# A 4-layer hybrid diffusion step in fp32 halves: the order of the products in the first blocks

## Chip, cores, metric

One Trainium2 chip, one core. The metric is the time of one execution of the program on the device, in microseconds, as the median over runs.

## What is computed

One inference step of 384 tokens (128 context tokens, 256 latent ones) with 1024 channels through four layers. Layer l mixes tokens with a bidirectional Mamba-2 scan (l = 0, 3), a gated short convolution (l = 1) or differential attention (l = 2), and then runs a gated convolutional FFN. Each half of a layer is normed before and after, and shifted, scaled and gated by a modulation vector:

```python
def sandwich_layer(x, mod, g, mix_fn, ffn_fn):
    sh1, sc1, gt1, sh2, sc2, gt2 = jnp.split(mod, 6, axis=-1)
    m, aux = mix_fn(rmsnorm(x, g[0]) * (1 + sc1) + sh1)
    x = x + gt1 * rmsnorm(m, g[1])
    f = ffn_fn(rmsnorm(x, g[2]) * (1 + sc2) + sh2)
    x = x + gt2 * rmsnorm(f, g[3])
    return x, aux

def conv_ffn(h, w_up, conv_w, w_down):
    u = dwconv(h @ w_up, conv_w)
    gate, val = jnp.split(u, 2, axis=-1)
    return (jax.nn.silu(gate) * val) @ w_down
```

The argument of mix_fn and ffn_fn is called h here.

## The kernel before

**Two parts.** Matrix products are made in a rounded 32-bit format. To keep the accuracy, every operand is split in two parts, a first part (its rounded value) and a second part (what the rounding left). A product is then three matmuls: first × first, first of the weight × second of h, second of the weight × first of h. The first part of h is hh, the second hl; those of a weight chunk are wh and wl.

**How h is made.** h is channel-major: two tiles of four 128-channel blocks for hh and two for hl, each over all 384 tokens. It comes in three token tiles of 128 (t = 0, 1, 2). For each, normed (line 278) makes the normalised tile xn, turned (288) transposes its eight blocks on TensorE, and modulated (298) scales and shifts them into h32, four blocks at a time: three on ACT (L309), the fourth on VectorE (L307). A cast on VectorE (L311) makes hh, and a subtraction (L312) makes hl. The second half's subtraction runs on POOL for t = 0 and 1; all others run on VectorE. There are HB = 2 buffers of h32 (four before layer 0).

**How weights come.** wplan lists all weight chunks in the order of use. ahead (141) loads them (four raw buffers wr), rounds a chunk on ACT (L155, wh) and subtracts on VectorE (L156, wl); WS = 4 chunks of parts are held. A chunk has 1024 columns: four channel blocks by two output blocks of 128 in the FFN, two chunks for a pair of output blocks; in the short convolution 768 columns, four chunks for three output blocks. dt of the scan has one chunk of 512 columns, all eight channel blocks by 64 outputs.

**Channel-major phases.** The scan's input projections, the short convolution's and the FFN's upward product write channels on the partitions and the 384 tokens along the free axis. cm_block (330) makes one output block: it goes through the chunks and channel blocks, and for each issues the three matmuls (L340) into one bank of PSUM, 24 in all (dt: 24 with 64 columns). FFN and short convolution have five banks (mm), the scan three and two (mm, yp). An FFN step (i = 0 to 21) makes two blocks, gate and value, each of which goes through conv (393: ACT L396, VectorE L398 and L400). The short convolution makes three blocks per step. The scan makes dt first (steps, 536), then pairs of blocks. Attention takes its projections token-major (L811) and does not use cm_block.

**What lies between phases.** tm_out (353) makes the product at the end of each half layer; as soon as a token tile is finished, it takes the residual, the norm and the next h for it, so the last tile's norm, transposes, h and cast stand between one phase's products and the next's. The modulation products (modps, L187) for later layers are spread over the program as filler on TensorE, and their weights (w_mod) come through the same DMA queue.

**What sets the order.** Everything is issued by one Python program, but the context is made with schedule_with_timeline_sim=True: at build time, instructions are put in order on each engine by an estimate of when their inputs are ready, with the program's order as priority. On the chip each engine then runs its list in order.

Of the kernel before, what the change touches and what calls it, by code (L numbers as in the profile page):

```python
# [10 lines left out]
F32 = mybir.dt.float32  # L11
# [3 lines left out]
ALU = mybir.AluOpType  # L15
# [4 lines left out]
P = 128  # L20
D = 1024
KB = D // P
T = 384
# [21 lines left out]
class Net:  # L45
# [252 lines left out]
    def modulated(self, l, which, t, trs):  # L298

        o, n = TOK[t]  # L300
        hh, hl = self._h4
        for hf, tr in enumerate(trs):
            h32 = self.op.tile([P, 4, P], F32, tag="h32", name="h32", bufs=self.hbufs)
            for b in range(4):
                A, B = self.ab(l, which, hf * 4 + b, COND[t])
                if b == 3:
                    self.V.tensor_scalar(h32[:, b, :], tr[:, b, :], A, B, op0=ALU.mult, op1=ALU.add)  # L307
                else:
                    self.S.activation(h32[:, b, :], tr[:, b, :], AF.Identity, scale=A, bias=B)  # L309
            hi, lo = hh[hf][:, :, o:o + n], hl[hf][:, :, o:o + n]  # L310
            self.V.tensor_copy(hi, h32)  # L311
            (self.GP if hf == 1 and t < 2 else self.V).tensor_tensor(lo, h32, hi.bitcast(F32), op=ALU.subtract)  # L312

    def gated(self, t, hf, acc, gt, parts):

# [15 lines left out]
    def cm_block(self, chunks, nblk, b, m=P, tag="mm"):  # L331

        acc = self.psum(tag)[:, :T]
        ops = []
        for k0, nk, hi, lo in chunks:
            for k in range(nk):
                o = (k * nblk + b) * m
                ops += [(hi[:, o:o + m], self.hh[k0 + k]), (hi[:, o:o + m], self.hl[k0 + k]), (lo[:, o:o + m], self.hh[k0 + k])]
        for n, (w, h) in enumerate(ops):
            self.PE.matmul(acc[:m], w, h, start=n == 0, stop=n == len(ops) - 1)  # L340
        return acc

    def cm_weights(self, nblk, m=P):
        per = max(1, 1024 // (nblk * m))
        out = []
        for k in range(0, KB, per):
            nk = min(per, KB - k)
            out.append((k, nk) + tuple(self.weights(nk * nblk * m)))
        return out
# [112 lines left out]
    def ffn(self, l, pl, then):  # L462
        d = self.d
        cw = pl.tile([P, 2 * NF, 3], F32, name="fcw")
        self.load(cw, d["ffn_conv"][l])
        g = [pl.tile([P, T], F32, name=f"fg{i}") for i in range(NF)]
        with self.tc.tile_pool(name=f"up{l}", bufs=1, reuse_waits="tile") as self.cpool:
            self.cbufs = 7
            for i in range(NF):
                ch = self.cm_weights(2)  # L470
                pg = self.cm_block(ch, 2, 0)
                pv = self.cm_block(ch, 2, 1)
                tg = self.conv(pg, cw[:, i])
                tv = self.conv(pv, cw[:, NF + i])
                self.S.activation(tg, tg, AF.Silu)
                self.V.tensor_tensor(g[i], tg, tv, op=ALU.mult)
                self.pace("ffn", i + 1, NF)

        def prep(k):
            hi = pl.tile([P, T], F32R, tag="gh", name="gh", bufs=RB)  # L480
            lo = pl.tile([P, T], F32R, tag="gl", name="gl", bufs=RB)
            self.split(g[k], hi, lo)
            return hi, lo

        self.tm_out(l, 1, NF, prep, then=then, room=1)

    def short(self, l, pl, then):
        d = self.d
        cw = pl.tile([P, KB, 3], F32, name="scw")
        self.load(cw, d["sc_conv"])  # L490
        hi = [pl.tile([P, T], F32R, name=f"sgh{i}") for i in range(KB)]
        lo = [pl.tile([P, T], F32R, name=f"sgl{i}") for i in range(KB)]
        self.cpool, self.cbufs = pl, 7
        for i in range(KB):
            ch = self.cm_weights(3)
            pc = self.cm_block(ch, 3, 0)
            pu = self.cm_block(ch, 3, 1)
            pb = self.cm_block(ch, 3, 2)
            cg = self.cpool.tile([P, T], F32, tag="c", name="cg", bufs=self.cbufs)
            self.S.activation(cg, pc, AF.Copy)  # L500
            self.V.tensor_tensor(cg, pu, cg, op=ALU.mult)
            t = self.conv(cg, cw[:, i])
            self.V.tensor_tensor(t, pb, t, op=ALU.mult)
            self.split(t, hi[i], lo[i])
            self.pace("mix", i + 1, KB)
        self.tm_out(l, 0, KB, lambda k: (hi[k], lo[k]), then=then, room=4)
# [31 lines left out]
    def steps(self, j, keep, pl, between):  # L538
# [4 lines left out]
        self.load(prm[:, 1], d["ssd_a_log"][j].partition_broadcast(P))  # L543
        na = pl.tile([P, 64], F32, name="na")
        wh, wl = self.weights(512)
        ps = self.cm_block([(0, KB, wh, wl)], 1, 0, 64)
        raw = pl.tile([64, T], F32, name="dtr")
        V.tensor_copy(raw, ps[:64])
        tr = self.pt.tile([P, 4, P], F32, tag="tp", name="tp")
# [30 lines left out]
        for dr, tri in ((0, self.Ur), (1, self.Lr)):  # L580
            ps = self.pt.tile([P, 512], F32, tag="tp", name="cum")
# [442 lines left out]
```

## Time and profile before

| | us |
|---|---|
| median of 3 runs | 2418.07 |
| lowest and highest run | 2415.47, 2423.82 |
| the profiled execution | 2415.22 |
| its span, first to last instruction | 2413.4 |
| TensorE (PE) busy | 2298.8 |
| VectorE (DVE) busy | 1618.8 |
| ScalarE (ACT) busy | 1252.9 |
| GpSimd (POOL) busy | 329.6 |

All times within the execution count from the start of the span. PE is TensorE's matmuls and PEld its weight loads, which overlap them; SP is the queue that issues DMAs. L340 is line 340 of the kernel before. Matmuls are pipelined, so their durations overlap: the distance of two starts is what one costs. mm<-hl,wh is a matmul that writes a tile mm and reads hl and wh. The mean granted clock of TensorE was 0.975 of full speed. The channel-major phases begin at 44.7 (scan of layer 0), 444.8 (its FFN), 741.2 (short convolution), 908.6 (its FFN), 1449.0 (FFN after attention), 1741.9 (scan of layer 3) and 2129.7 (its FFN).

### The profile page before, as it was taken

To read this page: it belongs to the slowest core of one execution; us is meant where nothing else is said; L and a number is where in the kernel's file an instruction comes from. 1 tells how busy PE (TensorE), PEld (TensorE's weight loads), DVE (VectorE), ACT (ScalarE), POOL (GpSimd) and SP (SyncE) were. 2 spreads that over 40 slices of the span, in tenths; PEclk is the share of its full clock that TensorE was granted. 3 is DMA by queue.
4 is the path that set the end of the run, shared out by engine and by line. 5 is a ranking of instruction groups with operands and counts; after the bars stand their busy time and mean duration, and the time that the engine had idled before them with its cause. 6 is when DMAs were issued, how large, how long until landed. Compare 5 with 4: busy or idle time off the path is not lost.

```text
span 2413.4 us, 35660 instructions
## 1 busy us (share of the span) xinstructions
PE 2298.8 (95%) x13132; PEld 2003.8 (83%) x13132; DVE 1618.8 (67%) x2930; ACT 1252.9 (52%) x2173; POOL 329.6 (14%) x498
## 2 busy tenths in 40 slices
PE   6989999899999999999999979999998999989998
PEld 3878887699977969998788649998687888779987
DVE  3887886677655457776655547776578888677765
ACT  3766765444444344444544444445556676554444
POOL 1222230100000010000133330000113223110000
PEclk7999999999999999999999989999999999989999
DMA  7656655533537563335435463345455654423342
GB/s 286 193 164 201 208 195 175 197 123 131 165 105 304 200 247 126 123 127 161 162 107 176 151 241 107 123 130 158 147 165 166 199 167 150 134 97 123 131 145 83
DMA packets 113375, 391.79 MB, mean 162 GB/s; under 512 B 13105, under 2 KB 25521, under 8 KB 100913
## 3 DMA queue, kind: packets, MB, share of 16 engines
q1 hardware_dynamic: 113200, 389.52, 48.7%
q8 instruction: 103, 1.69, 0.3%
q14 instruction: 72, 0.58, 0.1%
HBM read 382.39 MB, written 7.08 MB: 161 GB/s over the span
## 4 chain that ended last, share of the span: by engine, by line
PE 79%; DVE 9%; DMA 4%; ACT 2%; issue 2%; POOL 2%; SPq 0%; DVEq 0%; POOLq 0%; ACTq 0%
PE mm L340 44%; PE mm L380 20%; PE mm L811 5%; PE modps L187 2%; PE yp L380 2%; DVE e L686 2%; DMA wm<-in_w_mod 2%; DVE wl L156 1%; PE yp L726 1%; DVE w L690 1%; PE yp L852 1%; ACT jk L263 1%; DMA wx<-in_w_mod 1%; DVE cv L398 1%; DMA h<-in_state 1%
## 5 line engine op out<-in xcount | busy, mean ns | idle before, releaser
L340 PE MATMUL mm<-hh,wh 128*128 128x384 f32 (+1 forms) x2352 | 796.1, 340 | 15.2 <-DVE cv L400 9.5
L340 PE MATMUL mm<-hl,wh 128*128 128x384 f32 (+1 forms) x2352 | 793.9, 338 | 0.0
L340 PE MATMUL mm<-hh,wl 128*128 128x384 f32 (+1 forms) x2352 | 791.2, 338 | 0.0
L156 DVE TENSOR_TENSOR wl<-wr,wh 128x1024 fp32r<-128x1024 f32 (+2 forms) x466 | 564.0, 1212 | 259.7 <-ACT wh L155 257.6
L155 ACT ACTIVATE wh<-wr 128x1024 fp32r<-128x1024 f32 (+2 forms) x466 | 483.7, 1039 | 320.5 <-PE mm L340 258.2
L340 PEld LDWEIGHTS mm<-hh,wh 128*128 128x128 f32 (+1 forms) x2352 | 442.8, 189 | 38.8 <-DVE cv L400 14.5
L340 PEld LDWEIGHTS mm<-hl,wh 128*128 128x128 f32 (+1 forms) x2352 | 442.8, 188 | 4.6 <-issue 2.4
L340 PEld LDWEIGHTS mm<-hh,wl 128*128 128x128 f32 (+1 forms) x2352 | 442.2, 188 | 5.0 <-issue 3.3
L396 ACT ACTIVATE cv<-mm,fcw 128x384 f32<-128x384 f32 x176 | 100.1, 572 | 233.1 <-PE mm L340 228.2
L380 PE MATMUL mm<-wh,gh 128*128 128x512 f32 x528 | 208.7, 395 | 0.0
L380 PE MATMUL mm<-wl,gh 128*128 128x512 f32 x528 | 208.6, 395 | 0.0
L380 PE MATMUL mm<-wh,gl 128*128 128x512 f32 x528 | 207.9, 395 | 0.0
L271 POOL TENSOR_SCALAR m<-s 128x1 f32<-128x1 f32 x42 | 17.5, 417 | 1144.4 <-ACT jk L263 1143.6
L398 DVE SCALAR_TENSOR_TENSOR cv<-mm,fcw,cv 128x127 f32<-128x127 f32 x352 | 144.2, 410 | 42.6 <-ACT cv L396 42.6
L405 ACT ACTIVATE gh<-fg 128x384 fp32r<-128x384 f32 x176 | 92.1, 524 | 152.5 <-PE mm L380 151.6
L406 DVE TENSOR_TENSOR gl<-fg,gh 128x384 fp32r<-128x384 f32 x176 | 97.6, 557 | 96.8 <-ACT gh L405 96.1
L400 DVE SCALAR_TENSOR_TENSOR cv<-mm,fcw,cv 128x127 f32<-128x127 f32 x352 | 146.0, 416 | 10.8
L380 PEld LDWEIGHTS mm<-wh,gh 128*128 128x128 f32 x528 | 99.0, 187 | 24.8 <-issue 0.8
L380 PEld LDWEIGHTS mm<-wh,gl 128*128 128x128 f32 x528 | 99.0, 187 | 24.4
L380 PEld LDWEIGHTS mm<-wl,gh 128*128 128x128 f32 x528 | 99.0, 187 | 24.0
L187 PE MATMUL modps<-wm,sil 128*32 128x512 f32 x496 | 78.1, 654 | 15.7 <-DMA wm<-in_w_mod 14.7
L811 PE MATMUL mm<-wh,hh 128*128 128x256 f32 x288 | 83.4, 290 | 0.0
(224 smaller groups left out, 3169.0 us busy)
## 6 DMA issues: line engine op xcount, KB each, us to landing
wr<-in_ffn_up SPq DMA_DIRECT2D x176, 512.0 KB
wm<-in_w_mod SPq DMA_DIRECT2D x62, 1024.0 KB
wr<-in_ssd_in SPq DMA_DIRECT2D x96, 512.0 KB
wr<-in_ffn_down SPq DMA_DIRECT2D x88, 512.0 KB
wx<-in_w_mod SPq DMA_DIRECT2D x34, 1024.0 KB
ab<-acs SPq DMA_DIRECT2D x48, 512.0 KB
wr<-in_ssd_out SPq DMA_DIRECT2D x32, 512.0 KB
wr<-in_sc_in SPq DMA_DIRECT2D x32, 384.0 KB
```

The source lines that it names most:

```text
L155: self.S.activation(hi[:, :m], raw[:, :m], AF.Copy)
L156: self.V.tensor_tensor(lo[:, :m], raw[:, :m], hi[:, :m].bitcast(F32), op=ALU.subtract)
L187: self.PE.matmul(acc[32 * j:32 * j + 32, :], self.sil[:, kb, :], raws[:, j // 2, (j % 2) * 512:(j % 2 + 1) * 512], start=kb == 0, stop=kb ...
L340: self.PE.matmul(acc[:m], w, h, start=n == 0, stop=n == len(ops) - 1)
L380: self.PE.matmul(acc[t], g[:, o:o + n], w, start=k == 0 and i == 0, stop=k == nk - 1 and i == 2)
L396: self.S.activation(t, src, AF.Copy, scale=cw[:, 1:2])
L398: self.V.scalar_tensor_tensor(t[:, o + 1:o + n], src[:, o:o + n - 1], cw[:, 0:1], t[:, o + 1:o + n], op0=ALU.mult, op1=ALU.add)
L400: self.V.scalar_tensor_tensor(t[:, o:o + n - 1], src[:, o + 1:o + n], cw[:, 2:3], t[:, o:o + n - 1], op0=ALU.mult, op1=ALU.add)
L405: self.S.activation(hi, src, AF.Copy)
L406: self.V.tensor_sub(lo, src, hi.bitcast(F32))
L686: V.scalar_tensor_tensor(e[:, sl], abs_[t][:, 0, sl], dac[:, t, hs:hs + 1], abs_[t][:, 1, sl], op0=ALU.subtract, op1=ALU.min)
L811: PE.matmul(acc[t][:, :256], h[k][:, o:o + m], w[:, ws], start=k == 0 and i == 0, stop=k == KB - 1 and i == 2)
```

## The change

A new function cm_first makes all output blocks of a phase's first step together. It takes chunk by chunk, and in a chunk block by block, the products with hh (wh·hh, then wl·hh for each channel block); only then, block by block, all products with hl. It is used for dt in the scan, for step 0 of the FFN and step 0 of the short convolution. All other steps use cm_block as before. In modulated, the two subtractions of a token tile are issued after both casts instead of each behind its cast; this holds wherever h is made, ahead of attention too.

```diff
@@ modulated
         o, n = TOK[t]
         hh, hl = self._h4
+        subs = []
         for hf, tr in enumerate(trs):
...
             hi, lo = hh[hf][:, :, o:o + n], hl[hf][:, :, o:o + n]
             self.V.tensor_copy(hi, h32)
-            (self.GP if hf == 1 and t < 2 else self.V).tensor_tensor(lo, h32, hi.bitcast(F32), op=ALU.subtract)
+            subs.append((self.GP if hf == 1 and t < 2 else self.V, lo, h32, hi))
+        for e, lo, h32, hi in subs:
+            e.tensor_tensor(lo, h32, hi.bitcast(F32), op=ALU.subtract)
@@ new, after cm_block
+    def cm_first(self, chunks, nblk, m=P, tags=None):
+
+        accs = [self.psum((tags or ["mm"] * nblk)[b])[:, :T] for b in range(nblk)]
+        cols = lambda k, b: slice((k * nblk + b) * m, (k * nblk + b + 1) * m)
+        for k0, nk, hi, lo in chunks:
+            for b in range(nblk):
+                for k in range(nk):
+                    for w in (hi, lo):
+                        self.PE.matmul(accs[b][:m], w[:, cols(k, b)], self.hh[k0 + k], start=k0 + k == 0 and w is hi, stop=False)
+        for b in range(nblk):
+            for k0, nk, hi, lo in chunks:
+                for k in range(nk):
+                    self.PE.matmul(accs[b][:m], hi[:, cols(k, b)], self.hl[k0 + k], start=False, stop=k0 + k == KB - 1)
+        return accs
@@ ffn
-                pg = self.cm_block(ch, 2, 0)
-                pv = self.cm_block(ch, 2, 1)
+                pg, pv = self.cm_first(ch, 2) if i == 0 else [self.cm_block(ch, 2, b) for b in range(2)]
@@ short
-            pc = self.cm_block(ch, 3, 0)
-            pu = self.cm_block(ch, 3, 1)
-            pb = self.cm_block(ch, 3, 2)
+            pc, pu, pb = self.cm_first(ch, 3) if i == 0 else [self.cm_block(ch, 3, b) for b in range(3)]
@@ steps
-        ps = self.cm_block([(0, KB, wh, wl)], 1, 0, 64)
+        ps, = self.cm_first([(0, KB, wh, wl)], 1, 64)
```

## Rows read from the trace of the kernel before

**Rows 1.** The page, part 1: busy time of the engines and share of the span.
```profile
PE 2298.8 (95%) x13132; PEld 2003.8 (83%) x13132; DVE 1618.8 (67%) x2930; ACT 1252.9 (52%) x2173; POOL 329.6 (14%) x498
```

**Rows 2.** TensorE's waits: who waited for whom, us in total, times, longest.
```profile
PE tp L294 <- DVE xn L284: 21.1, 6, 7.2
...
PE mm L340 <- DVE hh L311: 5.7, 3, 2.8
```

**Rows 3.** Line L312: duration min/median/max in ns, then who waited for it (us, times).
```profile
L312 POOL TENSOR_TENSOR hl<-h,hh x16: 1264/1272/2133, 38.4 to 2128.0; 128x512 fp32r<-128x512 f32 x16
...
  ACT h L309: 8.8, 11
  PEld mm L340: 0.4, 1
```

**Rows 4.** Timeline, FFN 1's start: start, duration, engine, what [idle before <-releaser].
```profile
908.54 0.69 DVE L312 TENSOR_TENSOR hl<-h,hh 128x512 fp32r<-128x512 f32 x1
...
908.56 0.98 PE L340 MATMUL mm<-hh,wh 128*128 128x384 f32 x4
...
909.37 0.35 PE L340 MATMUL mm<-hl,wh 128*128 128x384 f32 x1
```

**Rows 5.** Timeline, start of the first scan phase.
```profile
44.70 1.22 PE L340 MATMUL mm<-hh,wh 128*64 128x384 f32 x3 [2.80 <-DVE hh L311]
...
46.43 0.18 PEld L340 LDWEIGHTS mm<-hl,wh 128*64 128x64 f32 x1 [0.38 <-DVE hl L312]
```

**Rows 6.** Stretch at FFN 3's start: length, then busy by engine; PEclk is the granted clock.
```profile
core 0: us, PE busy (x) PEld busy (x) DVE busy (x) ACT busy (x) POOL busy (x), PEclk, DMA share, GB/s
2129.80:2133.00 3.20, 3.20 (x10) 3.20 (x11) 2.03 (x4) 0.68 (x2) 0.00 (x0) 0.50 0.00 0
```

**Rows 7.** Timeline before the scan of layer 3: token tiles 1 and 2.
```profile
1738.62 0.69 DVE L312 TENSOR_TENSOR hl<-h,hh 128x512 fp32r<-128x512 f32 x1
1739.23 0.41 DVE L307 TENSOR_SCALAR h<-mm,cm 128x128 f32<-128x128 f32 x1
...
1739.43 1.16 ACT L309 ACTIVATE h<-tp,cm 128x128 f32<-128x128 f32 x3 [0.70 <-DVE hl L312]
1739.67 0.43 DVE L311 CAST hh<-h 128x512 fp32r<-128x512 f32 x1
...
1741.07 0.73 DVE L311 CAST hh<-h 128x512 fp32r<-128x512 f32 x1
...
1741.94 0.70 PE L340 MATMUL mm<-hh,wh 128*64 128x384 f32 x3 [0.80 <-DVE hh L311]
...
1742.80 0.41 DVE L307 TENSOR_SCALAR h<-tp,cm 128x128 f32<-128x128 f32 x1 [0.28 <-ACT h L309]
```

**Rows 8.** Timeline, VectorE, token tile 0 before the scan of layer 3.
```profile
1733.77 0.74 DVE L311 CAST hh<-h 128x512 fp32r<-128x512 f32 x2
```

**Rows 9.** Timeline, VectorE's xn twice before the scan of layer 3.
```profile
1729.64 0.51 DVE L284 TENSOR_SCALAR xn<-x,r 128x512 f32<-128x512 f32 x1 [1.08 <-POOL r L273]
...
1735.91 1.49 DVE L284 TENSOR_SCALAR xn<-x,r 128x512 f32<-128x512 f32 x1 [0.80 <-POOL r L273]
```

**Rows 10.** Timeline, short convolution: first products, next weights, second step's first wl.
```profile
741.19 0.81 PE L340 MATMUL mm<-hh,wh 128*128 128x384 f32 x3
...
751.21 2.44 ACT L155 ACTIVATE wh<-wr 128x768 fp32r<-128x768 f32 x3
...
756.08 0.33 PE L340 MATMUL mm<-hh,wl 128*128 128x384 f32 x1
```

**Rows 11.** Timeline, ACT in FFN 1's first step.
```profile
913.25 1.06 ACT L155 ACTIVATE wh<-wr 128x1024 fp32r<-128x1024 f32 x1 [4.61 <-PE mm L340]
916.37 0.58 ACT L396 ACTIVATE cv<-mm,fcw 128x384 f32<-128x384 f32 x1 [2.06 <-PE mm L340]
```

**Rows 12.** Layer 3's scan: VectorE copying dt out, then a piece of the chain.
```profile
1748.74 0.55 DVE L548 COPY dtr<-mm 64x384 f32<-64x384 f32 x1 [4.35 <-PE mm L340]
...
1763.48 4.16 PE mm L340 x24
```

## Prediction

> **What bounds the kernel now.** I read the page first. TensorE is busy for 95% of the span [rows 1], so this change pays only where TensorE stands still at the start of a channel-major phase. Then I read the waits of TensorE over the whole span, because they name what it stood still for [rows 2]. The largest wait at a boundary is not on h at all: it is 21.1 us for xn, the normalised last token tile, before it can be turned. For the first parts (hh, L311) TensorE's matmuls wait 5.7 us, three times. For the second parts (hl, L312) the list of TensorE's waits has no entry. The view of L312 says the same from the other side: of those who waited for a subtraction, TensorE has 0.4 us, once, in a weight load; the rest is 8.8 us of ACT, eleven times [rows 3]. That 0.4 us is the whole stall that the new order of products can remove directly.
>
> Why so little? Each accumulator takes its products in program order, but the kernel is built with an order that the build's own estimate of times chooses, and the trace shows what this does at a start. In FFN 1, TensorE issues four products hh·wh at 908.56, the first product of four accumulators, and the first product with hl at 909.37. Its hl began at 908.54 and took 0.69, so it was done at 909.23 [rows 4]. Four products at 0.17 us (24 in 4.16 us, [rows 12]) last until 909.24. The gap is 0.13 us. At the first SSD phase five products (three, then two of the other tag) bridge the same time at half the clock, and the 0.38 us of that weight load remain [rows 5]. [...] A phase therefore starts when the first part of token tile 2 is there, not when its second part is.
>
> **The change part by part.**
> *Work.* An accumulator still takes 8 blocks of h in 3 products each, so 24, and a pair of FFN blocks 48; weight loads, casts and subtractions are as many as before. Cost nothing.
>
> *Products with hl last.* This removes at most the 0.4 us of [rows 3]. I take −0.4.
>
> *The first accumulator is finished later.* In program order a pair's first accumulator ends with the 40th of 48 products instead of the 24th, 16 × 0.17 = 2.8 us later. In the trace FFN 1's first conv starts on ACT at 916.37, waiting for TensorE, 7.8 us or about 45 products after 908.56 [rows 4, 11]: the build already takes the products of both accumulators with the first half of h before those with the second half. So 40 is no later than what runs now. In the short convolution the first accumulator moves from the 24th to the 56th of 72, 5.5 us at most; what waits for it is ACT and VectorE, while TensorE has five banks and needs that bank only at its 120th product, 11 us after the 56th. Nothing; without free banks it would be those 5.5 us.
>
> *Weights are held longer.* The first part wh of a block is now read until the end. In FFN the first chunk is free after the 44th product instead of the 36th by program order; in FFN 1 the trace has ACT splitting the next chunk at 913.25, 4.7 us after the first product [rows 4, 11], and it would move to 908.56 + 44 × 0.17 = 916.0. That chunk is for the block pair after next, at the 97th product, 925: hidden with about 9 us to spare, less 1.06 for the split on ACT and some 1.2 on VectorE. In the short convolution four buffers are exactly one block. There the first chunk is free after the 66th product instead of the 54th, 741.19 + 66 × 0.17 = 752.4, and ACT starts splitting at 751.21 now, three in a row in 2.44 us [rows 10]. It moves by 1.2 us. The next block needs its first wl product at 756.08 [rows 10], but VectorE then also has the whole first conv in the same stretch. Between 0 and +1.5 us; I take +0.5, nearer the lower end because the row leaves more room than the move takes.
>
> *dt's accumulator* in both SSD phases gets all its hh products first. If its chain runs without a break it ends up to 2.6 us earlier (it is copied out at 1748.74, 6.8 us after 1741.94, and 24 products are 4.2 us); if the second half of h is what it waits for, then 16 products instead of 12 stand behind that, 0.7 us later. Neither is seen: behind dt, TensorE has a continuous queue of the phase's first projections to 1763.48 and beyond [rows 7, 12]. 0; without that cover it would be −2.6 to +0.7 in each phase.
>
> *The subtractions behind both casts.* This is DVE's and POOL's queue, at all eight places where h is made, attention's too. For token tile 2 it changes nothing that TensorE sees: the cast of the second half is not ready when the subtraction is (1742.80, when its last quarter is only being made, against a first-half cast done at 1741.80 [rows 7]), so an order by readiness keeps the subtraction where it is, and hl is now needed only at the 33rd product of an FFN. For tile 0, both casts already stand together at some boundaries [rows 8] (five of the 24 tiles in all). The tile that matters is 1. There are two buffers for h32, and ACT makes tile 2's first quarter only when the subtraction of tile 1 has let the buffer go: ACT waits 0.70 us for that subtraction at 1739.43, and it ends in the cast at 1741.07 for which TensorE waits 0.80 [rows 7]. If that subtraction goes behind L307 (0.41) and the cast (0.43) of the second half, with gaps some 0.88 in all, the start moves by as much. Four boundaries have this wait (short, attention, SSD 3, FFN 3), and at two of them (SSD 3 and FFN 3) TensorE waits for the cast behind it. So 0 to +1.8; I take the middle, +0.9, since the order is the build's choice and no row says which way it falls.
>
> [...] VectorE's xn takes 0.51 alone and 1.49 when it starts beside POOL's subtraction, and POOL's own goes from a median of 1.27 to 2.13 [rows 3, 9]. [...]
>
> *Sum.* −0.4 + 0.5 + 0.9 = +1.0 us. The profiled run took 2415.22 (span 2413.4), so 2416.2 against itself; the median of the three shown runs is 2.85 above it, which gives 2419.1, say 2419.0.
>
> **The rivals.**
> *A, the forecast: the stall was already bridged.* Terms at their ends give −3 to +4 us, and the shown runs lie 2.6 below to 5.8 above their median: 2413 to 2425. That the build keeps almost the old order of subtractions (the change doing nothing there) belongs to it, 2418.
>
> *B, slower: tile 1's first subtraction gets in ACT's way.* Place: between tile 1 and tile 2, at the four boundaries with ACT's wait. Price: 0.88 for standing behind the second cast, and 0.98 more when it meets POOL's subtraction there, 1.86 × 4 = 7.4 us, so 2425.5, say 2426. It decides from the point where tile 2's cast comes later than TensorE's other work at the boundary (the modulation products), 1.2 us of slack at the short convolution. For it: the ACT row of [rows 7]. Against it: two of the four have such slack. [...]
>
> *C, faster: h comes earlier.* If the reordered DVE queue brings tile 2's casts forward, all 5.7 us for hh [rows 2] and the 0.4 go: 2412, and about one more where a shorter pause spares products at a granted clock of 0.50 [rows 6]: 2411. For it: at the first SSD phase VectorE's queue sets the cast and TensorE waits 2.80 us [rows 5]. Against it: elsewhere ACT and the buffers set it.
>
> **How the numbers follow.** A 0.72, B 0.15, C 0.13. A is the likeliest, so 2419.0. To leave out no more than 2 in 10, the range reaches to most of B and C: 2409 to 2428. About 0.3% (7.3 us) is what a measurement can tell from no change; B is beyond it with 0.13 of its 0.15, C with 0.11 of its 0.13: faster 0.11, same 0.76, slower 0.13.
>
> **What the profile after would show.** Right: FFN's first products are hh·wh and hh·wl in long rows, hl starting after 32 of them; TensorE's waits still name xn first, hh about 5.7 us, L312 none; SSD 3 starts within 1 us of 1741.9 after its xn. Wrong: ACT's wait for hl at tile 2 grown from 0.70 to 1.5 or more (B), hh's waits below 3 us (C), TensorE standing for wh or wl in the short convolution's second block (my +0.5 too small), or a difference that lies away from the starts, in the SSD scans, which my sum does not hold.

## The result, and the profile after

The changed kernel took 2436.24 us in the median of six runs (2427.5 to 2439.87), the kernel before 2416.72 us beside it (2413.99 to 2423.82): a ratio of 1.0068, 95% interval [1.0054, 1.0081]. The change makes the kernel slower, by some 16 us as the ratio has it (the two medians lie 19.5 us apart), and the time lies outside the range of the forecast. The profiled execution of the changed kernel is the shortest of the six (2427.5 us, span 2425.7), so its trace holds 12.3 us of the loss; other kernels below, with the same order in their lists, show the rest.

The page's busy times, which answer to [rows 1]:

```profile
PE 2301.3 (95%) x13132; PEld 2004.7 (83%) x13132; DVE 1617.0 (67%) x2930; ACT 1245.8 (51%) x2169; POOL 330.4 (14%) x498
```

The work is the same, 13132 products. TensorE's waits for the last token tile (xn, hh) at the boundaries are no longer than in [rows 2]:

```profile
PE tp L294 <- DVE xn L284: 17.7, 5, 7.3
...
PE mm L354 <- DVE hh L312: 5.3, 3, 2.3
```

The line of the subtractions, L315 now, answers to [rows 3]; first the durations on POOL, then all who waited for it. TensorE's 0.4 us is gone from it, as the change means it to be; ACT's waits are 1.5 us longer in all:

```profile
L315 POOL TENSOR_TENSOR hl<-h,hh x16: 1262/1271/2125, 37.2 to 2139.9; 128x512 fp32r<-128x512 f32 x16
...
  ACT h L310: 10.3, 12
```

FFN 1's start, TensorE and ACT (start, duration, what, [idle before <-releaser]), answers to [rows 4, 11]. The first parts of h run in a row with wh and wl in turn. The first product with hl comes 3.2 us behind the first one, but it belongs to the second step (L343 is cm_block's line), which the build has put in between; the reordered pair's own products with hl (L358) begin 7.7 us behind it:

```profile
915.00 0.44 PE L354 MATMUL mm<-hh,wh 128*128 128x384 f32 x1
915.28 0.34 PE L354 MATMUL mm<-hh,wl 128*128 128x384 f32 x1
...
918.23 0.33 PE L343 MATMUL mm<-hl,wh 128*128 128x384 f32 x1
...
922.74 1.55 PE L358 MATMUL mm<-hl,wh 128*128 128x384 f32 x8
...
924.32 0.58 ACT L414 ACTIVATE cv<-mm,fcw 128x384 f32<-128x384 f32 x1 [9.24 <-PE mm L358]
```

The boundary before the scan of layer 3, same columns, answers to [rows 7, 12]:

```profile
1753.77 1.15 ACT L310 ACTIVATE h<-tp,cm 128x128 f32<-128x128 f32 x3 [0.70 <-DVE hl L315]
...
1756.28 0.36 PE L354 MATMUL mm<-hh,wh 128*64 128x384 f32 x1 [0.98 <-DVE hh L312]
...
1763.95 0.55 DVE L563 COPY dtr<-mm 64x384 f32<-64x384 f32 x1 [5.22 <-PE mm L358]
```

So TensorE's stall at the starts is gone as forecast, and yet this scan begins 14.3 us later than in [rows 7]. Where was it lost? I cut both traces at the first product with h of each phase (a phase so has its own output products and the next h at its end), and took the length, TensorE's busy time and the granted clock of each piece. In the windows view (length, busy by engine, PEclk) the kernel before, for the phases of scan 0, the attention and scan 3, and for one stretch in scan 0:

```profile
core 0: us, PE busy (x) PEld busy (x) DVE busy (x) ACT busy (x) POOL busy (x), PEclk, DMA share, GB/s
44.70:444.80 400.10, 374.61 (x2334) 318.54 (x2334) 309.29 (x590) 257.07 (x431) 97.28 (x107) 0.97 0.58 190
1198.40:1449.00 250.60, 234.93 (x1545) 181.10 (x1541) 124.45 (x257) 114.83 (x305) 79.90 (x181) 0.96 0.48 170
1741.90:2129.70 387.80, 362.77 (x2230) 317.12 (x2231) 302.98 (x587) 253.85 (x431) 99.10 (x107) 0.97 0.52 160
...
129.70:139.90 10.20, 7.08 (x44) 4.72 (x45) 8.73 (x23) 5.74 (x9) 1.04 (x1) 0.50 0.70 244
```

and the changed kernel:

```profile
43.50:449.90 406.40, 378.52 (x2334) 320.20 (x2334) 310.93 (x591) 254.50 (x429) 101.47 (x107) 0.96 0.58 187
1205.20:1464.50 259.30, 239.89 (x1544) 183.00 (x1540) 124.70 (x257) 114.34 (x304) 73.94 (x181) 0.95 0.46 162
1756.30:2141.50 385.20, 357.72 (x2231) 314.89 (x2231) 301.96 (x587) 250.87 (x428) 101.03 (x107) 0.98 0.54 161
...
129.00:146.10 17.10, 11.08 (x66) 7.88 (x67) 13.43 (x31) 8.49 (x16) 5.77 (x4) 0.50 0.67 220
```

Scan 0 is 6.3 us longer, the attention 8.7, scan 3 is 2.6 shorter; the other five phases are 1.1 longer together, and the stretch ahead of the first product is 1.2 shorter. (The 400.1 us of scan 0 are the shortest of all traces with the old order there; the other eight, of the kernels below, have 402.1 to 403.5 us.) The attention's products are not part of the edit at all, and the scans' are only in their first microseconds.

What had happened there is seen in the built programs, not in a time. The build orders each engine's list by its own estimate, and the two programs stand in different order far from the edit: 2104 of TensorE's 12078 places (418 of them in the stretches of the seven starts, the rest elsewhere), 477 of VectorE's 2930, 290 of ACT's 1922, 73 of POOL's 494, 81 of SP's 803. Hardly any lie in an FFN beyond its start; they are in scan 0, the short convolution, the attention and scan 3. Building each part by itself shows which part does it:

- The late subtractions alone change no place in any of the five lists. The build had them in that order already, so this half of the change is no change.
- The products at the four FFN starts change the lists there and around the third FFN's start; those of the short convolution change that phase's lists.
- The 24 dt products at each scan's start, alone, give scan 0, the attention up to its end, and scan 3 the order that the changed kernel has. They also move a few places at the short convolution.

### The profile page after: what moved, and what is told of

Its sections match the earlier page's. It is cut to its first block, busy times and chain, and to the rows that moved or that the text cites. A ratio compares the mean times of both kernels' runs of the same rounds, so it can differ in the third digit from the quotient of the medians.

```text
span 2425.7 us, 35657 instructions
## 1 busy us (share of the span) xinstructions
PE 2301.3 (95%) x13132; PEld 2004.7 (83%) x13132; DVE 1617.0 (67%) x2930; ACT 1245.8 (51%) x2169; POOL 330.4 (14%) x498
## 3 DMA queue, kind: packets, MB, share of 16 engines
HBM read 382.39 MB, written 7.08 MB: 161 GB/s over the span
## 4 chain that ended last, share of the span: by engine, by line
PE 77%; DVE 11%; DMA 3%; POOL 3%; issue 3%; ACT 3%; SPq 0%; POOLq 0%; DVEq 0%; ACTq 0%
PE mm L343 41%; PE mm L398 20%; PE mm L826 4%; PE modps L187 2%; PE yp L398 2%; DVE e L701 2%; PE mm L354 2%; DVE wl L156 2%; DVE w L705 2%; DMA h<-in_state 1%; PE yp L867 1%; PE yp L741 1%; DVE cv L416 1%; ACT jk L263 1%; POOL r L273 1%
## 5 line engine op out<-in xcount | busy, mean ns | idle before, releaser
L343 PE MATMUL mm<-hh,wh 128*128 128x384 f32 x2248 | 760.8, 339 | 12.5 <-DVE cv L418 12.5
L343 PE MATMUL mm<-hl,wh 128*128 128x384 f32 x2248 | 757.8, 337 | 0.0
L343 PE MATMUL mm<-hh,wl 128*128 128x384 f32 x2248 | 755.0, 337 | 0.0
L343 PEld LDWEIGHTS mm<-hh,wh 128*128 128x128 f32 x2248 | 422.8, 188 | 32.7 <-DVE cv L418 16.1
L343 PEld LDWEIGHTS mm<-hh,wl 128*128 128x128 f32 x2248 | 422.2, 188 | 4.8 <-issue 3.1
L343 PEld LDWEIGHTS mm<-hl,wh 128*128 128x128 f32 x2248 | 422.5, 188 | 3.1 <-issue 1.9
L187 PE MATMUL modps<-wm,sil 128*32 128x512 f32 x496 | 80.3, 655 | 15.5 <-DMA wm<-in_w_mod 14.6
L698 POOL TENSOR_TENSOR w<-cb,dt 128x512 f32<-128x512 f32 x48 | 76.1, 1597 | 92.2 <-DVE w L706 91.4
```

The lines of the kernel that those rows point to most:

```text
L187: self.PE.matmul(acc[32 * j:32 * j + 32, :], self.sil[:, kb, :], raws[:, j // 2, (j % 2) * 512:(j % 2 + 1) * 512], start=kb == 0, stop=kb ...
L698: GP.tensor_tensor(h4(w), cb[:, 1, t, None, :].to_broadcast([P, 4, P]), per(dt, 1), op=ALU.mult)
```

## The experiments

Two theories. **R, the rest of the lists:** the loss is the new order away from the starts. **S, the starts:** taking h's first part first costs it, and what comes later only looks different. To part them I needed the edit without the new order and the new order without the edit. For that a kernel gets a table with the order of each engine's list, and edges along it that fix the order alone and ask for no wait (the edit with the old lists is built with 2967 semaphore instructions on the five engines, the kernel before with 2971):

```
+def in_order(tc, nc, table):
...
+        for a, b in zip(order, order[1:]):
+            tc.add_manual_dep(mine[b], mine[a].name, keep, reason="in_order")
...
         build(tc, d)
+        in_order(tc, nc, TABLE)
```

A table mixes two orders by stretches: between two places up to which both lists hold the same instructions, either list's piece can stand. "The stretch of a start" is TensorE's piece that holds the reordered products of that start. All ratios below are to the kernel before, run beside it.

**The edit with the old lists.** The change, its seven starts as they are, everything else in the order of before.

> The whole change, with TensorE's list in the stretch of each of the seven starts as the changed kernel has it, and every other stretch of the five engines' lists held to the order of the kernel before by order-only edges. Theory R: the loss goes, because it lies in the other stretches; what stays is the starts, -1.2 us at the first and +1.2 at the short convolution: -2 to +3 us, a ratio of 0.999 to 1.0015. Theory S: the whole loss stays, 1.005 to 1.008.

Measured: 1.0001 [0.9992, 1.0011]. R. Its windows for the same three phases:

```profile
45.00:447.60 402.60, 376.85 (x2334) 320.06 (x2334) 310.50 (x591) 257.01 (x431) 99.04 (x107) 0.97 0.59 190
1200.50:1450.00 249.50, 234.21 (x1545) 181.05 (x1541) 124.59 (x257) 114.75 (x305) 78.61 (x181) 0.97 0.48 171
1742.90:2130.90 388.00, 361.60 (x2231) 315.56 (x2231) 302.94 (x587) 253.91 (x431) 99.11 (x107) 0.97 0.53 160
```

**The new lists without the edit.** The kernel before, its starts as before, everything else in the order of the changed kernel.

> The kernel before, its products in the order of before in the stretch of each of the seven starts, and every other stretch of the five engines' lists held to the order of the changed kernel by order-only edges. Theory R: the loss comes without the change, +9 to +20 us, a ratio of 1.004 to 1.008. Theory S: no loss, -2 to +3 us, 0.999 to 1.0015.

Measured: 1.0064 [1.0047, 1.0082]; R again. The windows:

```profile
43.40:451.70 408.30, 381.29 (x2335) 322.52 (x2335) 311.00 (x591) 254.75 (x429) 101.85 (x107) 0.96 0.58 187
1206.30:1470.70 264.40, 244.79 (x1545) 184.33 (x1541) 124.87 (x257) 114.67 (x304) 73.61 (x181) 0.93 0.45 159
1762.20:2147.60 385.40, 358.14 (x2231) 315.16 (x2231) 301.97 (x587) 251.10 (x428) 101.24 (x107) 0.98 0.53 161
```

Together the two settle it: the edit costs nothing that can be measured, the order has the whole loss. Read the two pairs of rows by column. In the attention the new order costs 14.9 us between these two kernels, more than between most others (see the end), 4.3 of it in time that TensorE stands idle (264.40 − 244.79 against 249.50 − 234.21) and 10.6 in longer busy time for the same number of products, at a granted clock of 0.93 against 0.97. In scan 0 it is 5.7 us, 1.3 idle and 4.4 busy.

**One part at a time, nothing held.** First the dt products alone, then all but them.

```
-        ps = self.cm_block([(0, KB, wh, wl)], 1, 0, 64)
+        ps, = self.cm_first([(0, KB, wh, wl)], 1, 64)
```

> The products with h's first part first at the two dt products alone (the starts of the two scan layers); the FFNs and the short convolution as before, the subtractions as before. Theory R (the rest of the lists): the build orders each engine's list by its own estimate, and this one edit already gives the lists of scan 0, of the attention and of scan 3 that the changed kernel has, hundreds of instructions away from the starts. The loss is there, so this kernel has most of it: scan 0 +5.3 us, attention and its output products some +7, scan 3 -2.5, about +8 to +12 us over before in the profile, a ratio of 1.004 to 1.007. Theory S (the starts themselves cost it): two of seven starts and 48 of 672 reordered products, which end no accumulator later than before, since there is one block alone: 0 to +2 us, a ratio of 0.999 to 1.001.

> The change without its part at the dt products: late subtractions, and the products with h's first part first at the four FFN starts and at the short convolution's. Theory R: the lists of both scans' bodies and of the attention's body are as before, so only what lies near those starts is left, short +1.2 us and something at the third FFN's start: -1 to +3 us, a ratio of 0.9995 to 1.0015. Theory S: five of the seven starts and 624 of the 672 reordered products, so nearly the whole loss: +8 to +15 us, 1.004 to 1.0065.

Measured: 1.0061 [1.0046, 1.0075] for the dt products alone and 1.0003 [0.9993, 1.0013] for the rest, as R has it. 48 of the 312 reordered products (24 at each scan, 48 at each FFN, 72 at the short convolution; the 672 and 624 of the expectations are a slip of mine) bring the loss with them.

**The same lists from another edit.** If R holds, an edit without the change's idea must do the same harm if the build answers it with the same lists. Putting only the dt products with wl last, with the two parts of h in turn as before, does that:

```
-        ps = self.cm_block([(0, KB, wh, wl)], 1, 0, 64)
+        ps = self.psum()[:, :T]
+        ops = [x for k in range(KB) for x in ((wh[:, k * 64:k * 64 + 64], self.hh[k]), (wh[:, k * 64:k * 64 + 64], self.hl[k]))] + [(wl[:, k * 64:k * 64 + 64], self.hh[k]) for k in range(KB)]
+        for n, (w, h) in enumerate(ops):
+            PE.matmul(ps[:64], w, h, start=n == 0, stop=n == len(ops) - 1)
```

> The kernel before with one edit that has nothing of the change's idea: in the two dt products the parts of h alternate as before, and only the products with the weights' second part come last. No order is held. The build nevertheless gives the changed kernel's lists in scan 0 on every engine, and nearly those in the attention and in scan 3. Theory R (the lists away from the starts hold the loss): most of it comes, +0.0018 for scan 0, about +0.004 for the attention, 0 to -0.001 for scan 3: a ratio of 1.004 to 1.0065. Rival S (taking h's first part first costs it): no difference, 0.999 to 1.001.

Measured: 1.0081 [1.0069, 1.0094], the loss and somewhat more than I had put down; its attention phase took 265.4 us. And the other way round, the whole change with a form of the dt products to which the build answers with nearly the old lists:

```
-        ps, = self.cm_first([(0, KB, wh, wl)], 1, 64)
...
+        for ks in (range(4), range(4, KB)):
+            ops += [(w[:, cols[k]], self.hh[k]) for w in (wh, wl) for k in ks]
+            ops += [(wh[:, cols[k]], self.hl[k]) for k in ks]
```

> The whole change with one word altered: the dt products take h's first part first within each half of h (eight products with the first part, four with the second, and so for the other half), not over all of h. No order is held; the build gives scan 0, the attention's body and scan 3 nearly the lists of the kernel before. Theory R: 0.999 to 1.0015, like the change without its dt part (1.0003). Rival S: 48 reordered products less eight a scan, so the loss stays, 1.004 to 1.007.

Measured: 1.0003 [0.9993, 1.0013]. The change can be had without the loss, and without holding any order, but it brings nothing either.

**Which phase.** The new order in one phase alone, on all five engines, the rest as before.

> The kernel before, with the changed kernel's order in scan 0 alone, from behind the dt products to the scan's output products, on all five engines; everywhere else, and at the start itself, the order of before. The traces give the first phase 400.1 us in the kernel before and 402.6 and 403.5 in the two runs with its lists, against 406.4 to 408.3 in the three with the changed lists: if each phase pays for its own list (theory L), +3 to +6 us, a ratio of 1.001 to 1.0025. If one phase's list costs only together with a later one's (theory T, a shift that is handed on), 0 to +2 us.

> The kernel before, with the changed kernel's order in the attention phase alone (its products, scores and values, its output products, up to the third FFN's start). The phase took 250.6, 249.5 and 253.2 us with the lists of before, 259.3, 263.0 and 264.3 with the changed ones, and the FFN behind it 1.0 to 1.4 less. Theory L (each phase pays for its own list): +7 to +12 us, a ratio of 1.003 to 1.005, the larger part of the loss. Theory T (a shift handed on from scan 0): 0 to +3 us, under 1.0015.

> The kernel before, with the changed kernel's order in scan 3 alone. The phase took 387.8 and 387.9 us with the lists of before and 385.2, 387.3 and 385.3 with the changed ones. Theory L: -0.5 to -2.5 us, a ratio of 0.999 to 1.000, the one place where the changed order is not worse, and a candidate to keep. Theory T: no difference.

Measured: 1.0018 [1.0010, 1.0027], 1.0044 [1.0028, 1.0060] and 0.9991 [0.9981, 1.0000]. Each phase pays for its own list: 0.0018 + 0.0044 − 0.0009 = 0.0053, within the interval of the new lists without the edit (1.0047 to 1.0082). No sign is seen that scan 0 hands anything on to the attention: with scan 0's new order alone, the attention's phase took 249.8 us.

**What in scan 0.** The first suspect was one load. In the kernel before (timeline; VectorE, SP's queue, TensorE) the modulation's weights wm leave at 126.64, 81.9 us behind the phase's first product, and TensorE waits for them right behind a long wait for w, an operand of the scan's products that VectorE makes:

```profile
124.97 1.21 DVE L156 TENSOR_TENSOR wl<-wr,wh 128x1024 fp32r<-128x1024 f32 x1
...
126.64 0.38 SPq L63 DMA_DIRECT2D wm<-in_w_mod  x1
...
130.07 1.12 PE L726 MATMUL yp<-w,xt 128*64 128x128 f32 x8 [5.53 <-DVE w L691]
133.94 1.94 PE L187 MATMUL modps<-wm,sil 128*32 128x512 f32 x8 [2.75 <-DMA wm<-in_w_mod]
```

In the changed kernel they leave 86.0 us behind it, the wait for w is cut in pieces, and the wait for wm comes at the end of them:

```profile
127.80 1.21 DVE L156 TENSOR_TENSOR wl<-wr,wh 128x1024 fp32r<-128x1024 f32 x1
...
129.47 0.38 SPq L63 DMA_DIRECT2D wm<-in_w_mod  x1
...
128.02 0.66 PE L741 MATMUL yp<-w,xt 128*64 128x128 f32 x8 [2.00 <-DVE w L706]
129.67 1.12 PE L741 MATMUL yp<-w,xt 128*64 128x128 f32 x8 [0.99 <-DVE w L706]
131.74 1.12 PE L741 MATMUL yp<-ab,h 128*64 128x128 f32 x8 [0.95 <-DVE ab L712]
...
137.39 1.93 PE L187 MATMUL modps<-wm,sil 128*32 128x512 f32 x8 [3.67 <-DMA wm<-in_w_mod]
```

Around these waits stands the stretch at a granted clock of 0.50 that the windows above end with: 10.2 us before, 17.1 us after, with TensorE busy for 7.08 and 11.08 us of it. At full clock those products would take about half (the starts of two of them lie 0.32 us apart in the stretch and 0.17 behind it), so by this estimate the stretch costs 2.0 us more. Two runs were to tell whether SP's order (there the load stands behind two stores of the state) or the compute engines' order makes the load late.

> The kernel before, with SP's list alone in the changed kernel's order in scan 0: 15 of its loads and stores stand elsewhere, among them a load of the modulation's weights that is issued behind the two stores of the state and not ahead of them. In the trace of the kernel before that load leaves 81.9 us behind the scan's first product, in the changed kernel 86.0 us, and TensorE's 2.7 us wait for it ends 89.2 us behind it, against 93.9; the half clock around it lasts 10.2 us against 17.1. Theory Q (SP's order sets scan 0's loss): +3 to +5 us, a ratio of 1.001 to 1.002, and a half-clock stretch of 13 us or more there. Rival: the compute engines' lists set it (the scan's weights and its products), and SP's order alone is worth 0 to +1 us.

> The kernel before, with the changed kernel's order in scan 0 on TensorE, DVE, ACT and POOL, and SP's list in the order of before. All five gave 1.0018 and 407.5 us for the phase; SP's alone 1.0008 and 406.1 us; the lists of before 402.1 to 403.5 us. Theory Q (the late load of the modulation's weights sets it): the load goes out early again, so 402 to 404 us for the phase and a ratio of 1.000 to 1.0008. Rival C (the compute engines' order sets it): 405 us or more and 1.001 to 1.002.

Measured: SP's order alone 1.0008 [0.9997, 1.0018], which decides nothing; all but SP's 1.0019 [1.0010, 1.0028], the whole of scan 0's loss. My theory that the loss needs SP's order fell. But SP's order alone makes the load late as well: in its trace wm leaves 86.5 us behind the phase's first product, behind the two stores, TensorE waits 5.19 us for it, and the phase took 406.1 us:

```profile
129.86 0.41 SPq L65 DMA_DIRECT2D wm<-in_w_mod  x1
...
138.45 1.93 PE L189 MATMUL modps<-wm,sil 128*32 128x512 f32 x8 [5.19 <-DMA wm<-in_w_mod]
```

In the kernel with all but SP's order, wm leaves 86.5 us behind the first product too. SP's waits there from 121 to 131 us (who, for whom, us in total, times, longest) name what holds the load although SP's own list is the old one:

```profile
SPq L65 <- DVE wl L158: 15.4, 2, 9.5
```

SP has a load of raw weights wr queued ahead of wm, and wr needs the buffer that VectorE's split wl frees. In the two traces above wl ends at 126.18 and 129.01 (start and duration), wr leaves at 126.20 and 129.04, wm at 126.64 and 129.47. The new order has that split behind two blocks of w, y and s, so it begins 84.3 us behind the phase's first product and not 80.3, and the load of wm goes 4.0 us later as well, with SP's new list and with its old one. (Over all traces the split begins 80.3 to 82.8 us behind it with the old order on all engines, and 84.3 to 86.0 us with the new one.) That the load goes with the split, where no store stands before it, is shown; that the whole 0.0018 comes from it is not, since the same order also cuts up the wait for w.

**What in the attention.** First TensorE's list alone, then the new order on all engines but only up to the middle of the output products.

> The kernel before with TensorE's list alone in the changed kernel's order in the attention phase; the other four engines keep the lists of before. The phase with all five lists of the changed kernel cost 1.0044. Theory T (TensorE's own order sets it: one unit of the modulation's products stands among the first projections and not among the last heads, and the heads' products stand between other cover): most of it, 1.003 to 1.005 or more, since the other engines' lists no longer fit. Rival V (the order of the softmax steps on POOL, DVE and ACT sets it): 0 to +2 us, 1.000 to 1.001.

> The kernel before, with the changed kernel's order in the attention phase up to the middle of its output products on all five engines, and the order of before from there to the third FFN's start. The whole phase's changed order gave 1.0044, and its trace has the twelve heads' last result 7.8 us later in the phase than the kernel before. Theory H (the heads set it): 1.003 to 1.0045. Rival E (the end sets it, where the modulation's last units stand ahead of the third FFN's start): 0 to +3 us, 1.000 to 1.0015.

Measured: 1.0163 [1.0149, 1.0177] and 1.0028 [1.0013, 1.0042]. The first says only that a list fits the other engines' lists: alone, it makes a kernel that is worse than either (TensorE waits 15.6 us for wm in the phase and 11.3 us for the heads' on). The second lies just under theory H's range (1.003 to 1.0045) and above rival E's, and its interval reaches into both. As it stands it puts some two thirds of the 0.0044 on the projections, the heads and the first half of the output products; that this is the larger part is likely, and not clear of noise. The heads' last result, ACT's oh, in the kernel before:

```profile
1408.58 0.47 ACT L888 ACTIVATE oh<-tp,gs 128x256 fp32r<-128x256 f32 x1 [1.81 <-PE tp L886]
```

and with the new order up to the middle of the output products:

```profile
1415.96 0.47 ACT L890 ACTIVATE oh<-tp,gs 128x256 fp32r<-128x256 f32 x1 [1.80 <-PE tp L888]
```

Counted from the phase's first product (1198.4 and 1198.9) that is 210.2 and 217.1 us. TensorE's waits in the phase, in the same two kernels, first before:

```profile
PE tp L886 <- DVE on L881: 3.0, 3, 1.6
...
PE yp L852 <- ACT p L858: 1.1, 2, 0.8
```

```profile
PE tp L888 <- DVE on L883: 4.9, 5, 1.6
...
PE yp L854 <- ACT p L860: 1.7, 2, 1.4
```

There are two more waits for the heads' normed results (on), and those for the softmax (p) are longer, some 2.5 us in all. Up to the heads' last result TensorE stands idle 1.9 us longer (7.21 against 5.27) and is busy 5.0 us longer (209.89 against 204.93), at a granted clock of 0.98 in both. Which move in the projections and the heads does it stays open.

**The two best together.** The change at its starts, scan 3 in the new order, the rest as before.

> The whole change at the seven starts, the lists of before elsewhere, but scan 3 in the changed kernel's order: the two that measured best, 1.0001 for the change at the starts with the lists of before and 0.9991 for scan 3's list. If phases add (theory L): 0.998 to 1.000, the best of the versions, and faster than both kernels if it is under 0.999. If they do not: 1.000 or more.

Measured: 0.9991 [0.9982, 1.0000], the same as scan 3's order alone without the change. It is the best version by its number, and not one that can be told from the kernel before at the 0.3% of the forecast.

## Why the prediction was wrong

*What bounds the kernel.* Right: the stall on hl was 0.4 us, it is gone, and the waits for xn and hh are no longer than they were.

*The starts.* The sum of +1.0 us agrees with what it covers: the edit with the old lists took 1.0001 [0.9992, 1.0011], −1.9 to +2.7 us. That does not prove the sum, since no change at all agrees as well and two of its three terms came to nothing. Its terms, one by one:

- Work, 0: right, 13132 products.
- Products with hl last, −0.4: the stall is gone, and no run parts so little from nothing.
- The first accumulator: I had it no later than now. That was wrong, since the build puts the second step's products in between: FFN 1's first conv comes 9.3 us behind the first product (924.32 − 915.00) against 7.8, but it costs nothing that is seen: with the old lists the phase took 290.0 us, against 289.8.
- Weights held longer, +0.5: with the old lists the short convolution's phase took 167.0 us, against 167.4 before. The changed kernel has 168.7, but the kernel with the dt products alone, where this phase's products are as before, has 168.3. No cost of this term is seen.
- dt's accumulator: I took 0, between −2.6 and +0.7. Its copy begins 7.7 us behind the scan's first product in layer 3 (1763.95 − 1756.28), against 6.8: +0.9, just over the upper end, in the direction for which I gave a reason (16 products, not 12, stand behind the second half of h); no run tests the reason. TensorE's queue covers it, as forecast: with the old lists scan 3 took 388.0 us, against 387.8.
- The late subtractions, +0.9: 0. The build's lists are the same with and without them, and ACT's wait for hl at tile 2 is 0.70 us as in [rows 7]. Rival B had nothing to stand on: no subtraction moved, so no run here tests the 0.98 us that it put on one meeting POOL's. The row that this was worked out from, xn's 1.49 us in [rows 9], is not of two subtractions either.
- Rival C: TensorE waits 5.3 us for hh, not under 3. Right to set it low. Its last microsecond, products spared a granted clock of 0.50 by a shorter pause, is shown by no run: at FFN 3's start 11 products begin at 0.50 (0.32 us from one start to the next) behind a wait of 2.1 us for hh in the kernel before, and 15 behind one of 2.0 us in the changed kernel.

*The step that failed* is the sum's border. I read in [rows 4] that the build sets the order by its own estimate, and then priced the change as if that order stayed the same everywhere but at the starts. That step has no term in the sum and no rival among A, B and C. My last sentence names it, a difference away from the starts, in the scans, which my sum does not hold, but I gave it no chance and no price. It was the whole result: the new lists without the edit cost 1.0064, some 15.5 us, and the edit with the old lists 1.0001. The loss sits in scan 0 and in an attention phase whose products the diff does not touch. And the dt products, which I put at 0 because TensorE's queue covers them, are what redraws the lists there.

*What is not settled.* What the build's estimate saw in the dt products. Later dt results go with redrawn lists where nothing is held (the change, the dt products alone, wl last), and earlier ones with the old lists (by halves, 6.6 us behind the first product in layer 3), but the estimate itself is in no trace. Nor is shown why the new order in scan 3 is better and the one in the attention worse; no idea of the change speaks for either.

## What to carry to other kernels

Where a build orders the engines' lists by an estimate, an edit in one place can be an edit everywhere: compare the order of all lists, before and after, ahead of any sum, and give a redrawn list a chance and a price of its own. When a time moves that the edit cannot explain, hold the lists and measure edit and order apart, in two kernels. And where one form of an edit redraws the lists and another does not, take the one that does not, or hold the better order.

## What the runs showed of the hardware

The larger part of what this order costs in the attention phase is not in TensorE's waits but in a longer busy time for the same number of products. Between the kernel with the new lists alone and the changed kernel with the old lists it is 4.3 us of idle time and 10.6 us of busy time. The stretches at a granted clock of 0.50 that begin in the phase add up to 37.5 us (6.8, 17.1, 6.8, 6.8) against 20.4 us (3.4, 6.8, 3.4, 6.8). Within the phase TensorE is busy for 31.4 and 15.1 us of all its time at 0.50; half of the difference, some 8 us, is an estimate of what the clock accounts for (by the starts above, 0.32 us apart at 0.50 and 0.17 behind it), and some 2.5 us of longer busy time are left without a cause. Just before the longest of them began, TensorE waited 1.0 and 0.5 us for the heads' results, one after the other (the window, then TensorE in the timeline):

```profile
1394.10:1411.20 17.10, 16.74 (x38) 9.28 (x39) 7.38 (x16) 7.77 (x26) 5.24 (x17) 0.50 0.09 32
...
1392.77 0.30 PE L888 MATMUL tp<-ident,on 128*128 128x128 f32 x1 [1.02 <-DVE on L883]
1393.60 0.33 PE L888 MATMUL tp<-ident,on 128*128 128x128 f32 x1 [0.53 <-DVE on L883]
```

This pair lies at the upper end of a spread that I had not expected. The five traces with the new order in the attention, wholly or up to its end, took 259.3, 259.9, 263.1, 264.4 and 265.4 us for the phase, with 23.8, 27.3, 30.6, 37.5 and 34.0 us of such stretches; the nine with the old order up to the heads' end took 247.3 to 253.2 us, with 13.6 to 27.2 us of them. So the lengths of the phase part the two orders, and the stretches at 0.50 alone do not: the kernel before has as many of them, 23.8 us, as the changed kernel. By the means of the five and the nine, the new order costs 12.4 us: 4.1 of idle time and 8.3 of busy time, of which the clock accounts for some 5.4 by the same estimate (25.6 against 14.9 us busy at 0.50). The profiled execution of the changed kernel has the shortest phase of the five, which goes with its being the shortest of its runs.
